# Issuing part of an attention layer's stores and loads from ScalarE's and GpSimd's queues in place of SyncE's

## The chip, the cores and the metric

The kernel runs on one core of one Trainium2 chip. The metric is the device time of one execution in microseconds (us); runs of this kernel took 2020.54 to 2025.85 us, with a median of 2025.57 us. Lower is better. Five engines with an instruction queue each work side by side: PE (TensorE, matrix products), DVE (VectorE), ACT (ScalarE), POOL (GpSimd) and SP (SyncE). An instruction queue is worked through in order: an instruction that waits holds up all that stand behind it on its engine. A transfer between the chip's HBM and the on-chip SBUF (a DMA) is started by an instruction on one of the queues and then runs by itself; whoever needs its data waits for its semaphore.

## What is computed

A stream of 1024 tokens with 1024 channels, float32, goes through two layers: an mLSTM layer (A) and a dilated attention layer (B), each followed by a residual and a layer norm. The change lies in layer B (and in the store of layer A's result that B's end reads). Layer B, from the reference, cut:

```python
def dilated_attention_layer(x, w_in, w_out, kv_blocks, slopes):
    proj = x @ w_in
    q_all = proj[..., :N_GROUPS_B * INNER_B].reshape(bsz, s, N_GROUPS_B, HEADS_B, HEAD_DIM_B)
    z = proj[..., N_GROUPS_B * INNER_B:]
    for g, (window, dilation) in enumerate(GROUPS_B):   # (128, 1), (512, 4), (2048, 16)
        qb = to_residue_blocks(q_all[:, :, g], dilation)
        kb, vb = kv_blocks[g]
        o, lse = dilated_block_attention(qb, kb, vb, dilation, window // dilation, slopes)
        outs.append(from_residue_blocks(o, bsz, s, dilation))
        lses.append(from_residue_blocks(lse, bsz, s, dilation))
    wts = jax.nn.softmax(jnp.stack(lses), axis=0)
    o = jnp.sum(wts[..., None] * jnp.stack(outs), axis=0).reshape(bsz, s, INNER_B)
    y = o.astype(x.dtype) * jax.nn.silu(z)
    return y @ w_out
...
        x = layer_norm(ALPHA * x + y, ln_g[layer], ln_b[layer])
```

There are 8 heads of 128 channels and three groups `g`, each with its own queries, keys and values. The three groups' outputs are merged with weights that come from their softmax denominators.

## The kernel before

Layer A takes the first 850 to 900 us, layer B the rest. Layer B's work is written as loops: `quad` 0 and 1 (heads 0 to 3, and 4 to 7), inside it the group `g` 0 to 2, inside it the head `h`.

Each float32 product is made by three matmuls (L97, L98, L99) on operands that are split into a high and a low part: ACT casts the high part (L92) and DVE subtracts it to get the low part (L93). The projections also go through a Strassen scheme, whose sums are made by DVE (L224, L230, L243, L247, L260, L261) and ACT (L1210 and others). So PE depends at every step on ACT's L92, DVE's L93 and DVE's L230.

The parts that the change touches, each with the tile or the HBM buffer that it moves:

- `layer_a_out` (L1001, L1050): stores layer A's normalized rows into `x1` (buffer `dx` in the order's rows), for layer B's residual.
- `residual(tb)` (L1079 to L1084): loads a block of `x1`, scales it, and stores it back.
- `values` (L1110, L1134): stores the values of a quad to `vn` (`dn`), and loads them back, regrouped, or for quad 1.
- `attend` (L1351): the attention of one head and one group. ACT copies its result out of PSUM into one tile, always the same buffer (L1346 or L1349, two copies), and the tile is stored to `og` (`dg`): 24 stores.
- `factors` (L1360 to L1368) and `merge` (L1383 to L1403): after a head's third group, softmax statistics go to HBM (`ds`), come back as six small loads, are turned into merge factors on DVE and ACT with 8 partitions, and are stored as `f` (`df`, L1403).
- `fetch` (L1405): loads the head's gate `z` (`dz`), the three `og` and the three `f`, each `f` row broadcast to 128 partitions (L1415). `combine` (L1424 to L1428, DVE) multiplies and adds them; `weigh` stores the result to `y2` (`dy`, L1461). For head 3 `by_group` (L1431) does this one group at a time.
- `gates` (L1476): stores the gate halves to `z2` (`dz`).

Weights come through `quarters` (L177) into two raw tiles that are used in turn, so that a weight load waits until DVE's L93 has read its tile for the last time. The output weights come at the end (L1544), with the loads of `y2` (L1546) beside them.

All transfers are issued from SP's queue, 640 in the whole program. The order of each engine's instructions isn't written out by hand: a scheduler lays them out with a simulated timeline when the program is built, within the data dependences and a few `issue_after` hints. So a change of the issuing queue also moves other instructions. SP and ACT share eight completion semaphores for their transfers, which are used in turn; a transfer that gets one again waits for that one's earlier transfer. Transfers of POOL have eight of their own.

Of the kernel before, what the change touches and what calls it, by code (L numbers as in the profile page):

```python
# [18 lines left out]
P = 128  # L19
SEQ = 1024  # L20
# [40 lines left out]
class Kernel:  # L61
# [887 lines left out]
    def layer_a_out(self):  # L949
# [36 lines left out]
        def norm(tbs):  # L986
            n = len(tbs)
            mv, x = self.variances([stats[tb] for tb in tbs])
            rstd = self.rstd(x, n, "ra")
            nb = self.t(self.cp, [P, n], tag="lnb1", bufs=4)  # L990
            V.scalar_tensor_tensor(nb, mv[:, :, 0], -1.0, rstd, op0=ALU.mult, op1=ALU.mult)
            for i, tb in enumerate(tbs):
                r, ri, ni = rows[tb], rstd[:, i:i + 1], nb[:, i:i + 1]
                if i % 2:
                    V.tensor_scalar(r, r, ri, ni, op0=ALU.mult, op1=ALU.add)
                else:
                    A.activation(r, r, AF.Identity, bias=ni, scale=ri)


                if tb >= 4:  # L1000
                    nc.sync.dma_start(self.dram["x1", tb], r)  # L1001

        def transposes(tbs, banks):

# [16 lines left out]
        for half in range(2):  # L1021
# [3 lines left out]
            for c in range(NC_A - tail):  # L1025
                y, w = stream(c, half), weights(c)

                late = c < 3 + half
                for i in range(3 if late else 4):
                    block(ps, i, c, y, w)  # L1030
                if late:
                    first.append((c, y, w))
                if c == 2 + half:
                    if half:
                        transposes((0, 1, 2, 3), Ring(6, 7))
                    else:
                        self.a_tail()
                    ps.append([self.bank(6 + dm) for dm in range(2)])
                    for part in first:
                        block(ps, 3, *part)  # L1040
                    if half:
                        gain, shift = self.ln_params(0, 12, 39)

                if half and c in (5, 6):
                    with self.tc.issue_after(self.last_split.ins):
                        self.x1[("11", "12")[c - 5]]
                if half and 7 <= c < 11:
                    with self.tc.issue_after(self.last_split.ins):
                        self.scale_row(rows[c - 7], gain, shift)
                    nc.sync.dma_start(self.dram["x1", c - 7], rows[c - 7])  # L1050
            if half:

                whs, wls, yhl = Ring(20, 21, 22, 23), Ring(24, 25, 26, 27), Ring(16, 17, 18, 19)
# [15 lines left out]
    def layer_b(self):  # L1069
# [9 lines left out]
        def residual(tb):  # L1079

            r = self.slot(52)
            nc.sync.dma_start(r, self.dram["x1", tb])
            self.scale_row(r, *gain0)
            nc.sync.dma_start(self.dram["x1", tb], r)  # L1084

        jt = self.const("jt", [P, 384], tag="k1")
        jt2 = self.const("jt2", [P, P], tag="k3")
# [9 lines left out]
        def values(g, quad):  # L1097
# [28 lines left out]
            def done(half, i, aps):  # L1126
# [4 lines left out]
                    v[half] = to[half, i]  # L1131
                if i or g:
                    for j, t in enumerate(to[half, i]):
                        nc.sync.dma_start(natural(rows(i, half))[:, 2 * j:2 * j + 2], t)  # L1134
                if g and i == 0:
                    load(half)

# [138 lines left out]
        def attend(h, g, sp, v):  # L1276
# [67 lines left out]
            for bank in range(2):  # L1344
                if g == 0:
                    A.copy(o[:, 512 * bank:512 * bank + 512], po[bank])  # L1346
                else:
                    r = 4 if g == 1 else 8
                    A.copy(o.rearrange("p (i r) -> p r i", r=r)[:, r // 2 * bank:r // 2 * bank + r // 2],  # L1349
                           po[bank].rearrange("p (r i) -> p r i", r=r // 2))  # L1350
            nc.sync.dma_start(self.dram["og", h, g], o)  # L1351

        def factors(h, stat):

# [49 lines left out]

        def fetch(h, accs, os, fbs, z=None):  # L1405

            os_ = [self.slot(accs if g == 0 else os) for g in range(3)]
            fbs_ = [self.slot(fbs) for _ in range(3)]
            if z is None:
                z = self.slot(os)  # L1410
                nc.sync.dma_start(z, self.dram["z2", h])
            for g in range(3):
                nc.sync.dma_start(os_[g], self.dram["og", h, g])
            for g in range(3):
                nc.sync.dma_start(fbs_[g], self.dram["f", h][g:g + 1, :].to_broadcast([P, SEQ]))  # L1415
            return os_, fbs_, z

        def combine(os_, fbs_, z, n=1):
# [12 lines left out]
        def by_group(h, acc, o, fb):  # L1431

            tiles = {}

            def load(g):
                tiles[g] = self.slot(o if g else acc), self.slot(fb)
                nc.sync.dma_start(tiles[g][0], self.dram["og", h, g])
                nc.sync.dma_start(tiles[g][1], self.dram["f", h][g:g + 1, :].to_broadcast([P, SEQ]))

            def step(g):  # L1440
                t, acc = tiles[g][0], tiles[0][0]
# [4 lines left out]
                    load(g + 1)  # L1446
                    return
                z = self.slot(fb)
                nc.sync.dma_start(z, self.dram["z2", h])
# [6 lines left out]
        def weigh(h, fetched):  # L1456

            with self.tc.issue_after(self.last_split.ins):
                acc = combine(*fetched)
            if h < 6:  # L1460
                nc.sync.dma_start(self.dram["y2", h], acc)  # L1461
            return acc

        gain0 = []
# [1 line left out]
        def gates(c2, slots, banks=ones, sz=None):  # L1466
# [4 lines left out]
            def done(half, i, aps):  # L1471
# [220 lines left out]
```

## Time and profile before

| | before |
|---|---|
| runs, us | 2020.54, 2025.57, 2025.85 |
| median, us | 2025.57 |
| profiled execution, us | 2023.8 |
| its span (first to last instruction), us | 2022.0 |
| mean granted TensorE clock | 0.996 of full speed |
| transfers, mean | 145 GB/s |

Busy time is given as a share of the span; PE's, DVE's, ACT's and POOL's shares and the windows of layer B are shown in the prediction. In the rows there, a tile in SBUF is written `s`, one in PSUM `b`, an HBM buffer begins with `d`, an input with `in_`; `x` and a number count instructions. In a row of the timeline the columns are start, duration, engine, line, operation, what it writes and reads, and, in brackets, how long the engine was idle before it and what ended that. `SPq` is SP's queue issuing a transfer. In a row of waits the columns are the total in us, the number of times, and the longest. A row of a window holds its length and then, for PE, PE's weight loads, DVE, ACT and POOL, the busy us and the instructions, then the granted clock, the share of the transfer engines and GB/s.

### The profile page before, as it was taken

How to read it: one execution, taken by the hardware profiler on the slowest of the kernel's cores; microseconds unless marked ns; L12 is line 12 of the kernel's file. 1: busy time of each engine (PE TensorE's matmuls, PEld its weight loads, DVE VectorE, ACT ScalarE, POOL GpSimd, SP SyncE). 2: the span in 40 equal slices, each digit the busy share in tenths (PEclk: the TensorE clock that was granted, in tenths of full speed). 3: DMA queues.
4: the chain of work that ended last, by engine and by line, in shares of the span. 5: the costliest groups of instructions: out<-in, count | busy, mean ns of one | idle time of the engine just before them, and what ended most of it. 6: DMA issues, size and time to landing. Idle time of an engine off the chain costs nothing. (4 is left out here: it accounts for less than half of the span.)

```text
span 2022.0 us, 26727 instructions
## 1 busy us (share of the span) xinstructions
PE 1969.0 (97%) x9576; PEld 1631.2 (81%) x9576; DVE 1451.8 (72%) x2867; ACT 1010.7 (50%) x2008; POOL 154.0 (8%) x127
## 2 busy tenths in 40 slices
PE   8999999999999999999999999999999999999897
PEld 6778888788888888878788888878877888888686
DVE  8778787675577776457867765776679877757878
ACT  5455555535645543343524542565554566765531
POOL 0110000012145343000000000000000000000000
PEclk9999999999999999999999999999999999999999
DMA  4345465456754543516121143224156322123753
GB/s 169 138 162 198 160 221 181 148 166 222 280 203 163 192 163 117 183 62 231 52 73 63 53 146 105 84 84 146 64 210 210 115 94 84 63 84 108 261 199 125
DMA packets 113148, 292.26 MB, mean 145 GB/s; under 512 B 13236, under 2 KB 31092, under 8 KB 113016
## 3 DMA queue, kind: packets, MB, share of 16 engines
q1 hardware_dynamic: 113016, 290.56, 41.1%
q8 instruction: 75, 1.23, 0.3%
q14 instruction: 57, 0.47, 0.1%
HBM read 202.13 MB, written 88.39 MB: 144 GB/s over the span
## 5 line engine op out<-in xcount | busy, mean ns | idle before, releaser
L98 PE MATMUL b<-s,s 128*128 128x512 f32 (+3 forms) x2720 | 1035.5, 382 | 3.0 <-DVE s L93 3.0
L97 PE MATMUL b<-s,s 128*128 128x512 f32 (+2 forms) x2720 | 1010.6, 386 | 28.0 <-ACT s L92 18.6
L99 PE MATMUL b<-s,s 128*128 128x512 f32 (+3 forms) x2720 | 1023.0, 383 | 4.9 <-DVE s L93 4.5
L92 ACT CAST s<-s 128x512 fp32r<-128x512 f32 (+3 forms) x706 | 436.5, 638 | 544.9 <-PE b L99 276.0
L93 DVE TENSOR_TENSOR s<-s,s 128x512 fp32r<-128x512 f32 (+3 forms) x702 | 508.2, 739 | 276.2 <-ACT s L92 272.6
L97 PEld LDWEIGHTS b<-s,s 128*128 128x128 f32 x2720 | 511.9, 188 | 134.6 <-ACT s L92 27.6
L99 PEld LDWEIGHTS b<-s,s 128*128 128x128 f32 x2720 | 511.1, 188 | 105.7 <-DVE s L93 10.2
L98 PEld LDWEIGHTS b<-s,s 128*128 128x128 f32 x2720 | 512.8, 189 | 99.3 <-DVE s L93 5.2
L230 DVE TENSOR_TENSOR s<-s,b 128x512 f32<-128x512 f32 x144 | 98.1, 682 | 37.8 <-PE b L99 35.6
L1273 ACT ACTIVATE s<-s,nmax 128x128 f32<-128x128 f32 (+1 forms) x192 | 84.3, 441 | 27.7 <-DVE nmax L1271 27.5
L224 DVE TENSOR_TENSOR s<-s,b 128x512 f32<-128x512 f32 x96 | 65.1, 680 | 19.9 <-PE b L99 16.4
L93 DVE TENSOR_TENSOR s<-b,s 128x512 fp32r<-128x512 f32 (+1 forms) x96 | 51.7, 553 | 33.9 <-ACT s L92 30.0
L558 DVE SCALAR_TENSOR_TENSOR s<-s,c_convw,s 128x512 f32<-128x512 f32 (+3 forms) x96 | 71.4, 755 | 3.1 <-ACT s L555 2.8
L802 ACT ACTIVATE s<-s,k 128x128 f32<-128x128 f32 x144 | 47.2, 392 | 42.2 <-DVE s L93 18.7
L243 DVE TENSOR_TENSOR s<-s,s 128x512 f32<-128x512 f32 x48 | 33.0, 688 | 42.9 <-DMA s<-in_w_xm 15.1
L1269 DVE CUSTOM_DVE_ANT_0 s<-b,k 128x128 f32<-128x128 f32 (+1 forms) x192 | 57.2, 346 | 3.5 <-PE b L99 3.2
L92 ACT CAST s<-b 128x512 fp32r<-128x512 f32 (+1 forms) x96 | 43.9, 480 | 21.9 <-PE b L99 14.5
L310 DVE TENSOR_TENSOR s<-s,s 128x1024 f32<-128x1024 f32 x32 | 40.1, 1253 | 20.1 <-DMA s<-in_w_o 9.9
L314 DVE TENSOR_TENSOR s<-s,b 128x512 f32<-128x512 f32 x80 | 50.7, 680 | 5.0 <-PE b L99 3.7
L1220 DVE SCALAR_TENSOR_TENSOR s<-s,s 128x512 fp32r<-128x512 f32 x48 | 42.3, 883 | 10.1 <-ACT s L1219 9.6
L761 POOL TENSOR_TENSOR s<-s 128x512 fp32r<-128x512 f32 x32 | 43.4, 1369 | 76.3 <-ACT s L760 68.8
L1287 PE MATMUL b<-c_ident,s 128*128 128x128 f32 x280 | 46.3, 277 | 2.0 <-ACT s L1273 1.9
(185 smaller groups left out, 1527.9 us busy)
## 6 DMA issues: line engine op xcount, KB each, us to landing
s<-in_w_qk SPq DMA_DIRECT2D x48, 512.0 KB
s<-in_w_out SPq DMA_DIRECT2D x40, 512.0 KB
dp<-s SPq DMA_DIRECT2D x32, 512.0 KB
s<-dp SPq DMA_DIRECT2D x32, 512.0 KB
s<-in_w_z SPq DMA_DIRECT2D x24, 512.0 KB
s<-in_w_v SPq DMA_DIRECT2D x24, 512.0 KB
dg<-s SPq DMA_DIRECT2D x24, 512.0 KB
s<-dg SPq DMA_DIRECT2D x24, 512.0 KB
```

The source lines that it names most:

```text
L92: self.nc.scalar.copy(h, src)
L93: self.last_split = (l_eng or self.nc.vector).tensor_tensor(l, src, f(h), op=ALU.subtract)
L97: mm(ps, lh, rh, start=start, stop=False, skip_group_check=skip)
L98: mm(ps, lh, rl, start=False, stop=False, skip_group_check=skip)
L99: mm(ps, ll, rh, start=False, stop=stop, skip_group_check=skip)
L224: V.tensor_tensor(o, p, q, op=add)
L230: V.tensor_tensor(o, p[lane][rows], q[lane][rows], op=add)
L314: V.tensor_tensor(o, p, q, op=add)
L558: V.scalar_tensor_tensor(u[i][:, lo:o + 512], xm[i][:, lo - s:o + 512 - s], convw[:, c, 3 - s:4 - s], u[i][:, lo:o + 512], op0=ALU.mult, o ...
L802: A.activation(E[:, i * P:i * P + P], src[:, i * P:i * P + P], AF.Exp, bias=self.bias[:, hd, ig, j:j + 1])
L1269: V.tensor_tensor_reduce(out=dst, in0=sc, in1=bias, op0=ALU.add, op1=ALU.max, scale=1.0, scalar=-3e38, accum_out=mx[:, b:b + 1])
L1273: self.last_exp = A.activation(res[b][0], res[b][0], AF.Exp, bias=nm[:, b:b + 1], accum_out=stat[:, 1, g, b:b + 1])
```

## The change

Layer B's stores, and the loads that wait for them, leave SP's queue. The `og` stores go to ACT's queue (24 transfers); the `x1`, values, `z2` and `y2` stores, the loads of `x1` in `residual`, of the values, and the fetches of `z`, `og` and `f` go to POOL's (106 transfers). The weights, the small tables of `factors` and `merge`, the fetch for head 7, and all that belongs to the end of the kernel stay on SP. In the new file the lines behind L1406 have a number higher by one. SP has 674 rows before and 544 now, POOL 132 and 238.

```diff
@@ layer_a_out
-                    nc.sync.dma_start(self.dram["x1", tb], r)
+                    nc.gpsimd.dma_start(self.dram["x1", tb], r)
...
-                    nc.sync.dma_start(self.dram["x1", c - 7], rows[c - 7])
+                    nc.gpsimd.dma_start(self.dram["x1", c - 7], rows[c - 7])
@@ layer_b, residual
-            nc.sync.dma_start(r, self.dram["x1", tb])
+            G.dma_start(r, self.dram["x1", tb])
             self.scale_row(r, *gain0)
-            nc.sync.dma_start(self.dram["x1", tb], r)
+            G.dma_start(self.dram["x1", tb], r)
@@ values
-                    nc.sync.dma_start(t, grouped(rows(quad, half))[:, 2 * j:2 * j + 2])
+                    G.dma_start(t, grouped(rows(quad, half))[:, 2 * j:2 * j + 2])
...
-                        nc.sync.dma_start(natural(rows(i, half))[:, 2 * j:2 * j + 2], t)
+                        G.dma_start(natural(rows(i, half))[:, 2 * j:2 * j + 2], t)
@@ attend
-            nc.sync.dma_start(self.dram["og", h, g], o)
+            A.dma_start(self.dram["og", h, g], o)
@@ fetch
+            queue = G if h < 7 else nc.sync
...
-                nc.sync.dma_start(z, self.dram["z2", h])
+                queue.dma_start(z, self.dram["z2", h])
             for g in range(3):
-                nc.sync.dma_start(os_[g], self.dram["og", h, g])
+                queue.dma_start(os_[g], self.dram["og", h, g])
             for g in range(3):
-                nc.sync.dma_start(fbs_[g], self.dram["f", h][g:g + 1, :].to_broadcast([P, SEQ]))
+                queue.dma_start(fbs_[g], self.dram["f", h][g:g + 1, :].to_broadcast([P, SEQ]))
@@ by_group: its four transfers, in the same way
-                nc.sync.dma_start(tiles[g][0], self.dram["og", h, g])
+                G.dma_start(tiles[g][0], self.dram["og", h, g])
...
@@ weigh
-                nc.sync.dma_start(self.dram["y2", h], acc)
+                G.dma_start(self.dram["y2", h], acc)
@@ gates
-                    nc.sync.dma_start(self.dram["z2", 2 * c2 + i][:, 512 * half:512 * half + 512], o)
+                    G.dma_start(self.dram["z2", 2 * c2 + i][:, 512 * half:512 * half + 512], o)
```

The scheduler's order moves with it. Three places follow; a name is a tile (`s`, `b`) or a buffer, with its number in the program.

On DVE, where head 5 is combined while head 6's projection and the last gate's splits run. `s_2665`, `s_2666` and `s_2667` are the three groups' outputs, `s_2668` and `s_2669` broadcast factors; `s_2715` is a Strassen sum that PE's next product reads, `s_2722` and `s_2745` are low parts. Before:

```order
L93 TENSOR_TENSOR s_2722_16445<-s_2710_16336,s_2722_16445 128x512
L1424 TENSOR_TENSOR s_2665_16080<-s_2665_16080,s_2668_16083 128x1024
L1359 COPY s_2694_16258<-b_2693_16256 48x128
L230 TENSOR_TENSOR s_2715_16342<-s_2715_16342,b_2714_16341 128x512
L93 TENSOR_TENSOR s_2745_16567<-s_2738_16558,s_2745_16567 128x512
L1424 TENSOR_TENSOR s_2666_16081<-s_2666_16081,s_2669_16084 128x1024
L1424 TENSOR_TENSOR s_2667_16082<-s_2667_16082,s_2670_16085 128x1024
L230 TENSOR_TENSOR s_2715_16342<-s_2715_16342,b_2713_16340 128x512
```

And now:

```order
L230 TENSOR_TENSOR s_2715_16342<-s_2715_16342,b_2714_16341 128x512
L93 TENSOR_TENSOR s_2722_16445<-s_2710_16336,s_2722_16445 128x512
L1425 TENSOR_TENSOR s_2665_16080<-s_2665_16080,s_2668_16083 128x1024
L93 TENSOR_TENSOR s_2745_16567<-s_2738_16558,s_2745_16567 128x512
L1425 TENSOR_TENSOR s_2666_16081<-s_2666_16081,s_2669_16084 128x1024
L230 TENSOR_TENSOR s_2715_16342<-s_2715_16342,b_2713_16340 128x512
L1425 TENSOR_TENSOR s_2667_16082<-s_2667_16082,s_2670_16085 128x1024
```

The first multiplication with a factor (L1424, now L1425) stood ahead of the first L230 and stands behind it now; the second L230 has two of the three multiplications ahead of it, where it had three.

On SP, where head 2's output is fetched (`s_2147`), head 1's result is stored (`dy_88`), and the next projection's weights are loaded (`s_2211`). Before:

```order
L1411 DMA s_2151_12852<-dz_96_161 128x1024
L1351 DMA dg_99_164<-s_2144_12818 128x1024
L1461 DMA dy_88_153<-s_2109_12606 128x1024
L1413 DMA s_2147_12848<-dg_99_164 128x1024
L177 DMA s_2211_13244<-in_w_qk 128x1024
L1476 DMA dz_110_175<-s_2187_13094 128x512
L1403 DMA df_101_166<-s_2138_12784 8x3x128
```

And now:

```order
L1364 DMA s_2138_12784<-ds_100_165 8x128
L1367 DMA s_2138_12784<-ds_100_165 4x4x32 x2
L177 DMA s_2211_13244<-in_w_qk 128x1024
L177 DMA s_2212_13246<-in_w_qk 128x1024
L1403 DMA df_101_166<-s_2138_12784 8x3x128
```

The store of `dg_99`, the store of `dy_88` and the fetch that waits for the first of them no longer stand ahead of the weights; what is left ahead are the small tables.

On ACT, where the same `dg_99` is stored now:

```order
L237 COPY s_2195_13104<-b_2191_13100 128x512
L92 CAST s_2199_13154<-s_2190_13098 128x512
L1349 COPY s_2144_12818<-b_2140_12796 128x4x128
L1351 DMA dg_99_164<-s_2144_12818 128x1024
L92 CAST s_2200_13175<-s_2189_13096 128x512
L1390 ACTIVATE s_2138_12784<-s_2138_12784 8x384
```

The store follows the second copy directly, and a split (L92) of the gate's weights stands behind it.

At the end of the kernel the load of the second layer norm's gain (L945) now stands ahead of head 6's six small loads, which stood ahead of it before; the first load of output weights (L1544, now L1545) follows behind three of them.

More of the change, by code (lines that the diff above doesn't have):

```diff
@@ L1436, in load @@
                 tiles[g] = self.slot(o if g else acc), self.slot(fb)
-                nc.sync.dma_start(tiles[g][0], self.dram["og", h, g])
-                nc.sync.dma_start(tiles[g][1], self.dram["f", h][g:g + 1, :].to_broadcast([P, SEQ]))
+                G.dma_start(tiles[g][0], self.dram["og", h, g])
+                G.dma_start(tiles[g][1], self.dram["f", h][g:g + 1, :].to_broadcast([P, SEQ]))
             def step(g):
@@ L1448, in step @@
                 z = self.slot(fb)
-                nc.sync.dma_start(z, self.dram["z2", h])
+                G.dma_start(z, self.dram["z2", h])
                 V.tensor_tensor(acc, acc, z, op=ALU.mult)
-                nc.sync.dma_start(self.dram["y2", h], acc)
+                G.dma_start(self.dram["y2", h], acc)
             load(0)
@@ L1460, in weigh @@
             if h < 6:
-                nc.sync.dma_start(self.dram["y2", h], acc)
+                G.dma_start(self.dram["y2", h], acc)
             return acc
```

## The prediction

> **What bounds the kernel now.** I read the page's shares first, then the windows of layer B, then the waits of each engine, and last the timeline around PE's gaps.
>
> ```profile
> PE 1969.0 (97%) x9576; PEld 1631.2 (81%) x9576; DVE 1451.8 (72%) x2867; ACT 1010.7 (50%) x2008; POOL 154.0 (8%) x127
> POOL 0110000012145343000000000000000000000000
> q1 hardware_dynamic: 113016, 290.56, 41.1%
> 1000.00:1200.00 200.00, 199.41 (x997) 168.55 (x998) 140.16 (x282) 92.13 (x208) 0.00 (x0) 1.00 0.21 74
> ...
> sum 1172.00, PE 1137.56 PEld 950.36 DVE 850.43 ACT 579.41 POOL 0.00; mean PE 162.51 PEld 135.77 DVE 121.49 ACT 82.77 POOL 0.00
> ```
>
> PE is busy 97% of the span. The change touches layer B, the stretch from 850 to 2022 us, where PE is busy 1137.56 of 1172.00 us: at most 34.4 us of PE's idle time lie there (a little more where a matmul's modelled end covers a gap), and part of that is the last rows of the kernel, after the last matmul. POOL, which gets most of the moved transfers, does nothing after slice 16, so its queue delays no arithmetic. The transfers use 41.1% of the sixteen DMA engines, so the question isn't bandwidth but when each one is issued. In what PE waits for in layer B, and what the others wait for there, these rows matter:
>
> ```profile
> PE b L97 <- ACT s L92: 7.5, 7, 3.2
> PE b L97 <- DVE s L230: 7.2, 5, 2.6
> DVE s L1424 <- DMA s<-df: 23.2, 6, 5.5
> ACT s L92 <- DMA s<-in_w_out: 28.6, 11, 7.0
> ACT s L92 <- DMA s<-in_w_qk: 8.3, 3, 3.5
> ```
>
> PE's own large waits are twelve, 7.5 + 7.2 = 14.7 us together: that is the prize if every late transfer came in time. SP's queue is full of waits, but most are no loss:
>
> ```profile
> SPq L177 <- DVE s L93: 415.2, 54, 19.4
> SPq L1134 <- DVE s L314: 72.8, 10, 40.5
> SPq L1351 <- ACT s L1349: 56.2, 11, 12.4
> SPq L1413 <- DMA dg<-s: 21.1, 7, 4.6
> SPq L1415 <- DMA df<-s: 9.0, 4, 3.5
> ```
>
> L177 loads the weights' quarters. 54 times it is at the head of the queue waiting for DVE's last read of its own buffer, so nothing ahead of it can have delayed it there. The moved instructions block SP for 72.8 us at L1134 and 56.2 us at L1351. The first lies around the values of groups 0 and 1, where PE is busy 199.41 of 200 us in the window 1000:1200: unblocking SP there can give nothing. So I look at PE's gaps one by one.
>
> **The change part by part.** *Merge factors and PE.* A head's `f` is stored (L1403), loaded back broadcast (L1415, three loads), and used by DVE (L1424). Twice that chain stops PE:
>
> ```profile
> 1505.32 0.29 SPq L1403 DMA_DIRECT2D df<-s  x1
> 1508.88 1.28 SPq L1415 DMA_DIRECT2D s<-df  x3
> 1512.93 1.22 DVE L1424 TENSOR_TENSOR s<-s,s 128x1024 f32<-128x1024 f32 x1 [4.57 <-DMA s<-df]
> 1514.07 0.68 DVE L230 TENSOR_TENSOR s<-s,b 128x512 f32<-128x512 f32 x1
> 1514.81 0.50 PE L97 MATMUL b<-s,s 128*128 128x512 f32 x1 [1.98 <-DVE s L230]
> 1883.15 1.27 SPq L1415 DMA_DIRECT2D s<-df  x3
> 1887.10 1.23 DVE L1424 TENSOR_TENSOR s<-s,s 128x1024 f32<-128x1024 f32 x1 [5.41 <-DMA s<-df]
> 1889.16 0.50 PE L97 MATMUL b<-s,s 128*128 128x512 f32 x1 [2.56 <-DVE s L230]
> ```
>
> DVE takes its work in order; L230, whose result PE needs, stands behind the L1424 that waits for `f`. The gaps are 1.98 and 2.56 us, 4.5 together. In the new order of DVE the first multiplication (now L1425) stands behind that L230 and one more L93, so PE gets its operand at once; but the next L230 is still behind the wait. With the same landing time DVE would be done with L1425 where it is done now, and PE, which has some matmuls in hand after the first L230, loses part of the gap only at the second. I take half: −2.3 us; bounds 0 and −4.5.
>
> *The landing time itself.* The row at 1883.15 shows three loads issued by SP in 1.27 us, 0.42 each; the first is used 4.0 us after its issue (1508.88 to 1512.93). What one transfer costs POOL's queue no row shows, since POOL issues none. From below it is SP's 0.42 us; from above the nearest row of POOL work:
>
> ```profile
> L761 POOL TENSOR_TENSOR s<-s 128x512 fp32r<-128x512 f32 x32 | 43.4, 1369 | 76.3 <-ACT s L760 68.8
> ```
>
> 1.37 us, 0.95 more. The first multiplication needs the first load only, so it is 0 to 0.95 us later in each of six heads (head 3 fetches group by group, head 7's loads stay on SP): 0 to 5.7 us if it all reached PE. I take half a microsecond, as SP's row is the nearer in kind, and cover it by the L230 (0.68 us) that now goes ahead: cost 0. Without that cover it is 6 × 0.5 = 3.0 us. By the Trainium skill ("DMA: Bandwidth & Descriptors", section "Specifications") the first byte comes after about 1 µs on GpSimd's path and about 0.6 µs on the path of SP and ScalarE; by that alone the six heads would be 6 × 0.4 = 2.4 us later, an estimate; no run shows it yet, and the sum doesn't use it.
>
> *SP's head of line.* The place where a moved transfer visibly stands ahead of weights that PE then misses:
>
> ```profile
> 1530.44 0.68 DVE L93 TENSOR_TENSOR s<-s,s 128x512 fp32r<-128x512 f32 x1
> 1531.19 0.32 SPq L1413 DMA_DIRECT2D s<-dg  x1
> 1531.60 0.38 SPq L177 DMA_DIRECT2D s<-in_w_qk  x1
> 1537.97 0.62 ACT L92 CAST s<-s 128x512 fp32r<-128x512 f32 x1 [2.47 <-DMA s<-in_w_qk]
> 1538.64 0.50 PE L97 MATMUL b<-s,s 128*128 128x512 f32 x1 [1.54 <-ACT s L92]
> ```
>
> L1413 waits there for a store, and L177 behind it goes at 1531.60. But L177's buffer is last read by the L93 that ends at 1530.44 + 0.68 = 1531.12. Freed of L1413 it goes 0.5 us earlier, not more: −0.5 of the gap's 1.54. The largest gap of all is like it:
>
> ```profile
> 1894.36 0.36 SPq L1413 DMA_DIRECT2D s<-dg  x1
> 1899.09 0.33 SPq L945 DMA_DIRECT2D s<-in_ln_g  x1
> 1899.85 0.32 SPq L1461 DMA_DIRECT2D dy<-s  x1
> 1900.27 1.94 SPq L1544 DMA_DIRECT2D s<-in_w_out  x1
> 1908.67 2.09 ACT L92 CAST s<-s 128x1024 fp32r<-128x1024 f32 x3 [7.02 <-DMA s<-in_w_out]
> 1910.29 0.50 PE L97 MATMUL b<-s,s 128*128 128x512 f32 x1 [3.23 <-ACT s L92]
> ```
>
> Here L1461 goes to POOL, and the output weights could be issued 1900.27 − 1899.85 = 0.4 us earlier. But L945, which stays on SP and waits for ACT until 1899.09, is still ahead of them, and in the new order three small loads of merge factors stand between the two (they were issued before L945). So I put this gap at 0, bounds −3.2 and +2. What is late after this change is thus still L945 and the broadcast `f`.
>
> *Stores on ScalarE.* 24 stores of the attention's output (L1351) go into ACT's order, each right behind the copy that fills the tile.
>
> ```profile
> 1524.77 1.14 ACT L1349 COPY s<-b 128x512 f32<-128x512 f32 x1
> 1525.94 0.32 SPq L1351 DMA_DIRECT2D dg<-s  x1
> 1526.98 0.52 ACT L1390 ACTIVATE s<-s 8x384 f32<-8x384 f32 x1 [1.07 <-DVE s L1389]
> ```
>
> On SP the store takes 0.32 us and starts 0.03 us after the copy's end. On ACT it also holds up the next instruction, which otherwise would follow at once: 0.35 us each, 24 × 0.35 = 8.4 us of ACT. ACT is busy 579.41 of 1172 us there, about half; so half, 4.2 us, falls where ACT would be idle anyway, as in the 1.07 us above. Of the other 4.2 us, what delays a split (L92) that PE waits for counts: PE waits for ACT as often as for DVE, so I take half again, +2.1 us. Bounds: 0, and 8.4 if every one reaches PE.
>
> *The rest.* The x1 stores and residuals, the values' stores and loads, z2 and y2 (L1001, L1050, L1082/1084, L1110, L1134, L1476, L1461) have no reader soon and leave SP, whose weights wait for their own buffers: 0, covered by PE's 199.41 of 200 us above. Their loads on POOL are in one order with the `f` loads, so a store that waits for DVE there can hold a fetch back, as it does on SP now: no change.
>
> **The sum.** −2.3 − 0.5 + 0 + 2.1 = −0.7 us. The profiled execution took 2023.8 us (1.8 around the span of 2022.0), the median of the runs is 2025.57, the lowest 2020.54. Forecast: 2023.8 − 0.7, about 2023 us. About 0.3%, 6 us, can be told from no change: faster means below 2019.5, slower above 2031.6.
>
> **The rivals.** *(A) The late transfers all go.* PE's two chains of gaps close, at 1514 and 1889 (4.5 us), at 1538 (1.5) and at 1910 (3.2), as SP is never blocked and DVE no longer stands before PE: −9.2 us, and −12 with the shorter gaps behind the same rows; 2012 to 2015 us. For it: each of these gaps names a transfer on SP. Against: L945 stays, and L177's buffer. *(B) Slower: `f` lands later than DVE's new order covers.* Place: the first L1425 of each of six heads, with the next L230 behind it. If a load costs POOL 1.37 us, the second of three, whose multiplication also stands ahead of an L230, is issued 2 × 0.95 = 1.9 us later than now. It decides from the point where the landing is more than 1.3 us later, the L230 and L93 (0.68 us each) that now go first. Price: at six heads 6 × 1.9 = 11.4 us, less where PE has work in hand (four of the six now), and ACT's stores on PE's path 2 to 8; 2030 to 2040 us. For it: the six waits for `f` are already 23.2 us long. Against: only two of the six reach PE. *(C) SP's issue time was never the bound, and the new queues give nothing:* 2023.8 to 2025.6 us, which stands within the forecast's range. The Trainium skill says the same ("DMA: Bandwidth & Descriptors", section "Issuing engines are not separate DMA queues"): whichever engine issues them, DMAs share the same sixteen engines, and other issuers only save the sequencer's time. The 54 waits of L177 agree with it. Apart from the named places, every engine's order in layer B is arranged anew by the scheduler, and this can move the time by some microseconds either way; it widens each case.
>
> **How the numbers follow.** Forecast with (C), 2019 to 2028 us: 0.44. (A), 2009 to 2019: 0.25. (B), 2028 to 2041: 0.31. Of the forecast's case 0.05 lies below 2019.5; of (A) 0.01 above it; of (B) 0.02 below 2031.6. Faster 0.29, same 0.42, slower 0.29. The likeliest case alone is 2019 to 2028. The range needs most of both rivals: 2010 to 2038 leaves out about 0.05 below and 0.1 above.
>
> **What would show it.** In the changed kernel: DVE's waits of L1425 for `f` (now 23.2 us, six; shorter speaks for A, above 32 for B); PE's waits for L230 (7.2) and for ACT's L92 (7.5: growing to 10 shows the price of the stores); the gap before the output weights (3.2, unchanged by my forecast); the length of a POOL issue against 0.42 us. I am wrong if PE gets new gaps at places not named here, from the new order alone, or if transfers on POOL land several microseconds later.

## The result, and the profile after

Runs of the changed kernel took 2036.80, 2040.38, 2041.03 and 2041.33 us, median 2040.7. With those of the kernel before (2016.81 to 2025.85, median 2023.05) the ratio is 1.0085 (95%: 1.0068 to 1.0101): slower by about 17 us. That is above the predicted range. The profiled execution took 2036.8 us, with a span of 2034.4 and a mean granted clock of 0.993. From the page of after, engines, POOL's slices, and the transfer queues:

```profile
PE 1971.4 (97%) x9576; PEld 1636.6 (80%) x9576; DVE 1451.3 (71%) x2867; ACT 1012.2 (50%) x2008; POOL 214.1 (11%) x233
POOL 0110000012145442000000001000011000000000
q1 hardware_dynamic: 92248, 225.54, 31.9%
q0 software_dynamic: 14496, 52.44, 7.4%
q10 hardware_dynamic: 3456, 12.58, 1.5%
```

The transfers now stand in three queues: q0 for POOL's, q10 for ACT's, q1 for SP's. In the traces SP issued 696 transfers before (not 640, as the part on the kernel before has it) and issues 566 now. PE idles 2034.4 − 1971.4 = 63.0 us, where it idled 2022.0 − 1969.0 = 53.0. Of the span's 12.4 us more, 10.0 are idle time of PE and 2.4 matmuls that took longer (the clock 0.993 after 0.996). Three windows of after, then of before (length, PE, PE's weight loads, DVE, ACT, POOL, clock, transfers):

```profile
1400.00:1600.00 200.00, 190.86 (x948) 158.12 (x947) 153.76 (x340) 105.24 (x216) 19.57 (x35) 0.99 0.42 141
1840.00:1960.00 120.00, 105.12 (x506) 86.92 (x505) 93.79 (x203) 63.15 (x120) 9.55 (x18) 0.94 0.63 223
1960.00:2034.00 74.00, 63.54 (x281) 52.26 (x279) 57.13 (x151) 8.37 (x8) 0.00 (x0) 0.96 0.26 96
```

```profile
1400.00:1600.00 200.00, 194.18 (x959) 161.41 (x958) 154.41 (x342) 104.98 (x215) 0.00 (x0) 0.99 0.41 141
1840.00:1960.00 120.00, 112.50 (x546) 92.29 (x546) 97.40 (x206) 60.25 (x116) 0.00 (x0) 0.99 0.64 230
1960.00:2022.00 62.00, 51.18 (x225) 41.72 (x223) 50.51 (x140) 8.31 (x8) 0.00 (x0) 0.94 0.28 102
```

From 1400 to 1600 us PE idles 9.14 us after 5.82, and from 1840 to the end 25.34 after 18.32: together 10.3 us more, so PE's added idle time lies in the two stretches where heads are merged. In the waits from 850 us on (total, times, longest):

```profile
PE b L97 <- ACT s L92: 14.7, 5, 6.9
PE b L97 <- DVE s L230: 2.1, 4, 0.8
DVE s L1425 <- DMA s<-df: 21.0, 6, 5.8
ACT s L92 <- DMA s<-in_w_out: 35.3, 15, 5.4
POOL s L1416 <- DMA df<-s: 28.7, 4, 14.8
SPq L177 <- DVE s L93: 703.2, 62, 42.2
```

PE's waits for L230 fell from 7.2 to 2.1 us, as the order on DVE promised. Its waits for ACT's L92 doubled from 7.5 to 14.7, most of it in two new gaps, at 1559 and 1956 us:

```profile
1555.70 0.62 ACT L92 CAST s<-s 128x512 fp32r<-128x512 f32 x1 [8.92 <-DVE s L260]
1559.39 0.51 PE L97 MATMUL b<-s,s 128*128 128x512 f32 x1 [4.31 <-ACT s L92]
1931.84 0.26 SPq L1403 DMA_DIRECT2D df<-s  x1
1932.89 0.84 SPq L1545 DMA_DIRECT2D s<-in_w_out  x2
1933.86 1.66 POOL L1416 DMA_DIRECT2D s<-df  x3 [14.81 <-DMA df<-s]
1943.37 1.23 DVE L1425 TENSOR_TENSOR s<-s,s 128x1024 f32<-128x1024 f32 x1 [5.84 <-DMA s<-df]
1954.46 1.99 ACT L92 CAST s<-s 128x1024 fp32r<-128x1024 f32 x2 [5.33 <-DVE s L1425]
1956.50 0.79 PE L97 MATMUL b<-s,s 128*128 128x512 f32 x1 [6.88 <-ACT s L92]
```

Read the last six rows as a chain: head 6's `f` is stored (L1403), SP issues two quarters of the output weights, POOL issues the three loads of `f`, and DVE can use the first 9.51 us after its issue (1933.86 to 1943.37; in the kernel before 6.27, with no wait). Two more multiplications, then ACT casts and PE waits 6.88 us. But the late transfer isn't the whole of it. Head 6's `f` is itself stored 12.5 us later than in the kernel before (1931.84 after 1919.35), and the run p2 below, which has the new order with every transfer on SP, has gaps of 4.34 and 5.53 us at the same two places. SP itself is freer than before: L177 waits 703.2 us for its own buffers, after 415.2.

In the changed kernel, operations that issue a transfer on POOL and on ACT, and the time from issue to landing of L1416 (`f`):

```profile
L1416 POOL DMA_DIRECT2D s<-df x18: 528/528/539, 1477.8 to 1935.0; - x18
DMA to landing us min/median/max: 4.0/7.3/13.4
L1351 ACTq DMA_DIRECT2D dg<-s x24: 326/326/352, 1109.2 to 1935.0; - x24
```

An issue takes POOL 0.53 us and ACT 0.33; the landing takes up to 13.4 us, in which the head's other `f` loads in the same queue have a part.

### The profile page after: what moved, and what is told of

Its sections match the earlier page's. It is cut to its first block, busy times and chain, and to the rows that moved or that the text cites. A ratio compares the mean times of both kernels' runs of the same rounds, so it can differ in the third digit from the quotient of the medians.

```text
span 2034.4 us, 26767 instructions
## 1 busy us (share of the span) xinstructions
PE 1971.4 (97%) x9576; PEld 1636.6 (80%) x9576; DVE 1451.3 (71%) x2867; ACT 1012.2 (50%) x2008; POOL 214.1 (11%) x233
## 3 DMA queue, kind: packets, MB, share of 16 engines
q1 hardware_dynamic: 92248, 225.54, 31.9%
## 5 line engine op out<-in xcount | busy, mean ns | idle before, releaser
L92 ACT CAST s<-s 128x512 fp32r<-128x512 f32 (+3 forms) x706 | 436.9, 637 | 536.7 <-PE b L99 285.2
L230 DVE TENSOR_TENSOR s<-s,b 128x512 f32<-128x512 f32 x144 | 98.1, 682 | 49.1 <-PE b L99 46.3
L1273 ACT ACTIVATE s<-s,nmax 128x128 f32<-128x128 f32 (+1 forms) x192 | 84.4, 441 | 33.9 <-DVE nmax L1271 33.3
L243 DVE TENSOR_TENSOR s<-s,s 128x512 f32<-128x512 f32 x48 | 33.1, 690 | 43.6 <-DMA s<-in_w_qk 14.7
L92 ACT CAST s<-b 128x512 fp32r<-128x512 f32 (+1 forms) x96 | 44.0, 480 | 20.6 <-PE b L99 14.2
L872 POOL TENSOR_TENSOR s<-s,s 128x512 f32<-128x512 f32 x32 | 42.7, 1351 | 64.0 <-DVE s L871 48.8
```

The lines of the kernel that those rows point to most:

```text
L92: self.nc.scalar.copy(h, src)
L230: V.tensor_tensor(o, p[lane][rows], q[lane][rows], op=add)
L1273: self.last_exp = A.activation(res[b][0], res[b][0], AF.Exp, bias=nm[:, b:b + 1], accum_out=stat[:, 1, g, b:b + 1])
```

## The experiments

The change does two things at once: it moves transfers to other queues, and the scheduler, seeing other queues, lays out every engine anew. To hold one still, a kernel was **pinned** to another's order: a table of instruction numbers per engine, and for each two neighbours a dependence that orders the issue and adds no wait.

```python
for a, b in zip(names, names[1:]):
    tc.add_manual_dep(at[b], a, kind, reason="in_order")   # kind: NoSync
```

On each queue the transfers then stand in the order in which they stood in the other kernel; between two queues nothing is fixed. Ratios are to the kernel before, on the same chip; they come from several runs, and the spans of single profiles scatter by some us around them. Rows, waits and landing times come from one profiled execution of each kernel.

### The queues, or the new order

All of the change, in the order of before (p1: the changed kernel, pinned), and no change of queues, in the order of the changed kernel (p2: the kernel before, pinned). The edit is the same for both, with different tables:

```diff
         Kernel(tc, aps, out).build()
+        in_order(tc)
```

> All moved transfers on their new queues, but every other instruction of PE, DVE, ACT and POOL, and the transfers within each queue, held in the order of the kernel before. Theory 'queues' (a transfer from POOL lands later, a store on ACT holds ACT up): the loss is still there, ratio to before 1.006 to 1.010. Theory 'order' (the scheduler's new order, above all head 6's statistics copied behind head 5's combination, so that head 6's factors come 12 us later): the loss is gone, ratio 0.997 to 1.002. Both: in between.

> All transfers on SP as before, but PE, DVE, ACT and SP held in the order of the changed kernel. Theory 'queues': ratio to before 0.997 to 1.002. Theory 'order': ratio 1.005 to 1.010.

p1: 1.0096 (1.0075 to 1.0117). p2: 1.0053 (1.0035 to 1.0070). So the new queues cost about 20 us by themselves. The new order, on the old queue, costs 11 us too, mostly in gaps like those at 1559 and 1956 above, which p2 has at 1565.73 and 1955.60:

```profile
1562.04 0.62 ACT L92 CAST s<-s 128x512 fp32r<-128x512 f32 x1 [10.59 <-DVE s L260]
1565.73 0.80 PE L97 MATMUL b<-s,s 128*128 128x512 f32 x1 [4.34 <-ACT s L92]
1955.60 0.79 PE L97 MATMUL b<-s,s 128*128 128x512 f32 x1 [5.53 <-ACT s L92]
```

So either part alone loses, but the two don't add: on the new queues the new order (1.0085) is no worse than the old (1.0096). And PE's waits for L92 are 14.3 us in p2, with every transfer on SP: a sum like the changed kernel's 14.7 comes from the order alone.

### Which of the moved transfers

Each in the order of before: only the `og` stores on ACT (p3), only POOL's transfers (p4), only the `f` loads on POOL (p5), POOL's transfers without the `f` loads (p6). And, with the scheduler free, the whole change but for the `f` loads (e3).

```diff
  # p3
-            nc.sync.dma_start(self.dram["og", h, g], o)
+            A.dma_start(self.dram["og", h, g], o)
  # p4: the changed kernel, with
-            A.dma_start(self.dram["og", h, g], o)
+            nc.sync.dma_start(self.dram["og", h, g], o)
  # p5: the kernel before, with
-                nc.sync.dma_start(fbs_[g], self.dram["f", h][g:g + 1, :].to_broadcast([P, SEQ]))
+                (G if h < 7 else nc.sync).dma_start(fbs_[g], self.dram["f", h][g:g + 1, :].to_broadcast([P, SEQ]))
  # p6: p4, and e3: the changed kernel, each with
-                queue.dma_start(fbs_[g], self.dram["f", h][g:g + 1, :].to_broadcast([P, SEQ]))
+                nc.sync.dma_start(fbs_[g], self.dram["f", h][g:g + 1, :].to_broadcast([P, SEQ]))
```

(`by_group`'s `f` loads, for head 3, go with the others.)

> The order of the kernel before, only the 24 og stores moved to ACT. My prediction's term: +2.1 us, ratio 1.001; if every store reaches PE, +8.4 us, ratio 1.004. Theory 'order': no more than 1.001.

> The order of the kernel before, the 106 transfers moved to POOL, the og stores left on SP. Theory 'queues' by way of POOL: ratio 1.004 to 1.010, with the first multiplication of each head (L1425) waiting longer for f than the 23.2 us of before, above 32 us. Theory 'order': 0.997 to 1.002.

> The order of the kernel before; only the broadcast loads of f (21 of the 24, all but head 7's) go from SP to POOL. Theory 'f' (POOL's f loads land later, DVE waits in front of what PE needs): most of the 1.1% that all POOL moves cost, ratio 1.006 to 1.011, DVE's waits for f above 32 us. Rival 'the other moves' (the loads of z, og and values, or the stores, are late or crowd the weights): ratio 0.999 to 1.003.

> The order of the kernel before; the moves to POOL without the f loads (85 transfers). Theory 'f': ratio 0.999 to 1.003. Rival 'the other moves': 1.006 to 1.011.

> The changed kernel, f loads back on SP, the scheduler free to order it. It puts head 6's statistics ahead of the small norm load again, as before. Theory 'f' (with the order a consequence of it): ratio 0.998 to 1.002. Rival: it stays above 1.005.

| kernel | ratio | 95% |
|---|---|---|
| p3, og stores on ACT | 1.0003 | 0.9989 to 1.0017 |
| p4, all of POOL's | 1.0110 | 1.0084 to 1.0136 |
| p5, only f on POOL | 1.0053 | 1.0036 to 1.0071 |
| p6, POOL's without f | 1.0015 | 0.9996 to 1.0035 |
| e3, all but f | 1.0011 | 0.9998 to 1.0024 |

The stores on ACT cost nothing that can be told. The `f` loads, 18 transfers and three for head 3 of the 130 moved, cost 11 us alone; without them the kernel is 0.15% (p6) or 0.11% (e3) above the one before, at most 0.35% by the intervals. In e3 only the queue of `f` differs from the changed kernel, and with it the scheduler's order: head 6's `f` is stored at 1914.49 there, and no gaps of 4 us or more stand at the two places. So the changed kernel has its new order as a consequence of where `f` is issued. p5 (+0.53%) and p6 (+0.15%) don't add up to p4 (+1.10%): together they cost about 8 us more than apart (1 to 16 with the three intervals taken as independent). One cause of that is visible, in p4 at head 0:

```profile
1476.61 0.27 SPq L1403 DMA_DIRECT2D df<-s  x1
1481.77 0.56 POOL L1414 DMA_DIRECT2D s<-dg  x1 [5.78 <-ACT s L1273]
1482.37 1.68 POOL L1416 DMA_DIRECT2D s<-df  x3
```

The last `og` load stands ahead of `f` in POOL's queue and still waits, probably for the store that it reads (issued at 1476.08; the row names ACT's L1273 and doesn't tell). So `f` goes 5.76 us after its own store; in the kernel before it was 3.63 (1472.29 to 1475.92). Head 4 is the same (5.32 after 3.73).

In p5 nothing stands ahead of `f` on POOL. The waits of its profile:

```profile
DVE s L1424 <- DMA s<-df: 36.7, 10, 6.6
PE b L97 <- ACT s L92: 10.5, 5, 5.2
PE b L97 <- DVE s L230: 9.7, 4, 4.1
```

The loads are issued, but land later. Head 1 in p5, and then the one row of the kernel before that the prediction doesn't show:

```profile
1507.93 0.29 SPq L1403 DMA_DIRECT2D df<-s  x1
1511.01 0.33 SPq L177 DMA_DIRECT2D s<-in_w_z  x1
1511.98 1.57 POOL L1415 DMA_DIRECT2D s<-df  x3 [33.27 <-DMA df<-s]
1517.59 1.23 DVE L1424 TENSOR_TENSOR s<-s,s 128x1024 f32<-128x1024 f32 x1 [6.61 <-DMA s<-df]
1519.47 0.69 PE L97 MATMUL b<-s,s 128*128 128x512 f32 x1 [4.13 <-DVE s L230]
```

```profile
1510.20 0.43 SPq L177 DMA_DIRECT2D s<-in_w_z  x1
```

Before, a weight quarter (L177) was issued at 1510.20, right behind the three `f` loads at 1508.88: one queue, and `f` stood first. In p5 nothing holds that quarter on SP, and it goes at 1511.01, 0.97 us ahead of the first `f` load. `f` is used 5.61 us after its issue, where it was 4.05, and PE's gap there is 4.13 after 1.98. So a new theory: it is not POOL that is slow; `f` has **lost its place ahead of the weights**, with which it shares the transfer engines. The rival: POOL's path itself is slower.

### Lost place, or slow path

The weight quarter moved ahead of `f` on SP, at heads 1, 2 and 5, with nothing on POOL (p11); `f` on POOL as in p5, with the quarter behind it made to wait until the last `f` load has landed (p12 at six heads, p14 at the five but head 6, whose `f` stays on SP); `f` on ACT's queue in place of POOL's (p13; head 3's `f` stays on SP there). All in the order of before.

```diff
  # p11, SP's order at head 1
+L177 DMA s_2190_13098<-in_w_z 128x1024
 L1415 DMA s_2112_12609<-df_94_159 128x1024
 L1415 DMA s_2113_12610<-df_94_159 128x1024
 L1415 DMA s_2114_12611<-df_94_159 128x1024
-L177 DMA s_2190_13098<-in_w_z 128x1024
  # p12, p14: behind in_order
+    for load, factor in BEHIND:
+        tc.add_manual_dep(at[f"I-{load}"], f"I-{factor}", wait, reason="behind_f")
  # p13
-                nc.sync.dma_start(fbs_[g], self.dram["f", h][g:g + 1, :].to_broadcast([P, SEQ]))
+                (A if h < 7 else nc.sync).dma_start(fbs_[g], self.dram["f", h][g:g + 1, :].to_broadcast([P, SEQ]))
```

> The kernel before, all on SP, its own order, but at heads 1, 2 and 5 the weight load that stands behind the three f loads in SP's queue stands ahead of them. Theory 'overtaking' (f is late on POOL because the weights no longer queue behind it): f is used 1 to 2 us later at these heads though POOL has no part in it, ratio 1.001 to 1.004. Theory 'path' (POOL's own transfers are slower): f not later by more than 0.5 us, ratio 0.999 to 1.001.

> Only the f loads on POOL in the old order, and the next weight load of SP at heads 0, 1, 2, 4, 5 and 6 waits until the last f load has landed, so no weights stand beside them. Theory 'overtaking': first use of f 4.0 to 4.5 us after its issue, most of the 0.53% comes back, ratio 1.000 to 1.003 (less if the weights are then late themselves). Theory 'path': first use stays above 5 us after the issue, ratio 1.004 to 1.007.

> The order of the kernel before, the f loads (but head 7's) issued by ACT. To read landing times: another queue beside SP's, but issued as SP's are. Theory 'path': first use about 4.0 us after the issue at heads 1 and 5, as on SP. Theory 'overtaking': 5 to 6 us, as on POOL. The time itself rises, since ACT waits for f's store ahead of its own work: ratio 1.003 to 1.012.

> As the run with f on POOL and SP's next weight load waiting for it (1.0064), but head 6's f stays on SP and nothing waits there, since in that run the wait I added held head 7's small loads and an output weight in SP's queue for 10 us. Theory 'overtaking': f on POOL by itself is then nearly free, ratio 1.000 to 1.003, no gap of 5 us before the last products of head 7's part. If the path by itself cost the time: 1.004 to 1.007.

From the rows of each timeline, the time from the issue of the first `f` load to DVE's first use of it, in us; at these heads DVE waits for it, so that it is the landing, except at head 2 of after, where DVE came later and 5.90 is only an upper bound:

| head | before | after | p5 (POOL) | p11 (SP, weights first) | p12 (POOL, weights wait) | p13 (ACT) |
|---|---|---|---|---|---|---|
| 1 | 4.05 | 4.85 | 5.61 | 5.99 | 4.31 | 5.45 |
| 2 | 3.86 | 5.90 | 6.49 | 5.11 | 4.14 | 6.04 |
| 5 | 3.95 | 5.30 | 5.15 | 6.01 | 4.40 | 4.26 |
| ratio | 1 | 1.0085 | 1.0053 | 1.0029 | 1.0064 | 1.0019 |

Head 1 in p11, then in p12:

```profile
1510.01 0.33 SPq L177 DMA_DIRECT2D s<-in_w_z  x1
1510.70 1.27 SPq L1415 DMA_DIRECT2D s<-df  x3
1516.69 1.23 DVE L1424 TENSOR_TENSOR s<-s,s 128x1024 f32<-128x1024 f32 x1 [6.71 <-DMA s<-df]
1518.57 0.79 PE L97 MATMUL b<-s,s 128*128 128x512 f32 x1 [4.34 <-DVE s L230]
```

```profile
1506.97 1.56 POOL L1415 DMA_DIRECT2D s<-df  x3 [30.95 <-DMA df<-s]
1511.28 1.23 DVE L1424 TENSOR_TENSOR s<-s,s 128x1024 f32<-128x1024 f32 x1 [5.28 <-DMA s<-df]
1513.16 0.50 PE L97 MATMUL b<-s,s 128*128 128x512 f32 x1 [1.87 <-DVE s L230]
1513.80 0.33 SPq L177 DMA_DIRECT2D s<-in_w_z  x1
```

p11 makes the lateness of p5 with all of it on SP: 5.99 us and a gap of 4.34, by one swap. p12 takes it away with `f` on POOL: 4.31 us and a gap of 1.87. For the landing at these heads both are measured: place in the queue, 1.3 to 2.1 us (p11 less before); POOL's path, 0.26 to 0.45 us (p12 less before; there nothing of SP's follows `f` at once, so the path may cost a little more). One quarter is 512 KB, 1.5 us at the 345 GB/s that after reached from 1934 to 1943.3 us, so the swap costs about one quarter's transfer, an estimate.

For the time it is settled in part. p11 is 1.0029 (1.0016 to 1.0043): three swaps alone make about 6 (3 to 9) of the 11 us of p5. But p12, where `f` lands in time, is 1.0064 (1.0046 to 1.0082), and p14 1.0041 (1.0027 to 1.0055): by what was expected of them, these times speak for the slow path, though the landing times speak against it. In both the added wait holds SP itself: in p12 at head 6 the output weights come late, and ACT's L92 waits 10.71 us for them at 1938.96; in p14 the quarter at head 1 goes at 1516.74 (before: 1510.20), and PE's waits for L92 are 12.2 us (before: 7.5). In these two runs a wait in another queue was no substitute for a place in the same one. What remains of p5 beside the three swaps can't be split further from these runs; one visible part is its head 6, whose loads share the transfer engines with the output weights (DMA share 1.03 from 1937 to 1943 us) and are used 5.7, 9.1 and 12.3 us after the first issue.

p13 is 1.0019 (1.0007 to 1.0032), below the 1.003 that was expected at least. Issued by ACT on a third queue, `f` is late at heads 1 and 2, where SP issues a quarter 0.39 and 0.19 us ahead of it, and on time at head 5 (4.26), where the quarter goes 2.23 us behind it. In that trace's packet records the first packet of `f` starts 1.93 and 2.72 us after its issue at heads 1 and 2, and 0.98 at head 5; in the kernel before it was 0.95 to 1.08. So what delays the landing is the weights nearby, with POOL or without it.

In the changed kernel `f` is late at head 5 though its first load is issued 0.44 us ahead of the quarter. The rows, and then each queue's packets, MB and share of the transfer engines, from 1890.5 to 1892.5 us (POOL's queue alone) and from 1892.5 to 1894:

```profile
1889.26 1.60 POOL L1416 DMA_DIRECT2D s<-df  x3 [5.18 <-DMA df<-s]
1889.70 0.36 SPq L177 DMA_DIRECT2D s<-in_w_z  x1
1894.56 1.22 DVE L1425 TENSOR_TENSOR s<-s,s 128x1024 f32<-128x1024 f32 x1 [4.89 <-DMA s<-df]
```

```profile
q0 software_dynamic: 103, 0.42, 100.8%
```

```profile
q1 hardware_dynamic: 75, 0.31, 53.8%
q0 software_dynamic: 40, 0.10, 35.5%
```

POOL's queue had moved 0.42 MB, less than its first load (0.52), when the weights came in with 0.31 MB to its 0.10. Being issued first did not protect `f` here, on a queue of its own.

### Can an order cover it?

The L230 that PE needs put ahead of the waiting L1424 at heads 1 and 5, queues as before (p7, the prediction's first term by itself); needed work put first at heads 0, 1, 2, 4 and 5 (p8); p8's order with `f` on POOL (p10); p4 with `f` ahead of the `og` load in POOL's queue (p9).

```diff
  # p7, DVE's order of before at head 1, and the same at head 5
+L230 TENSOR_TENSOR s_2160_12870<-s_2160_12870,b_2159_12869 128x512
 L1424 TENSOR_TENSOR s_2109_12606<-s_2109_12606,s_2112_12609 128x1024
-L230 TENSOR_TENSOR s_2160_12870<-s_2160_12870,b_2159_12869 128x512
  # p8 and p10, the same place
-L1424 TENSOR_TENSOR s_2109_12606<-s_2109_12606,s_2112_12609 128x1024
 L230 TENSOR_TENSOR s_2160_12870<-s_2160_12870,b_2159_12869 128x512
 L1359 COPY s_2138_12784<-b_2137_12782 48x128
 L93 TENSOR_TENSOR s_2196_13105<-s_2189_13096,s_2196_13105 128x512
+L1424 TENSOR_TENSOR s_2109_12606<-s_2109_12606,s_2112_12609 128x1024
...
  # p9, POOL's order at head 0
-L1414 DMA s_2075_12368<-dg_85_150 128x1024
 L1416 DMA s_2076_12369<-df_87_152 128x1024
 L1416 DMA s_2077_12370<-df_87_152 128x1024
 L1416 DMA s_2078_12371<-df_87_152 128x1024
+L1414 DMA s_2075_12368<-dg_85_150 128x1024
```

> The kernel before, all on SP, in its own order, but with the L230 that PE waits for put ahead of the first multiplication with f at heads 1 and 5. My prediction's term: 2.3 us less, bounds 0 and 4.5; ratio 0.9978 to 1.0. If the gap only moves to the next L230: 1.000.

> The kernel before, all on SP, its own order, but on DVE at heads 0, 1, 2, 4 and 5 the sums, low parts and the next head's statistics that PE's products wait for are put ahead of the multiplications that wait for f, and the third multiplication behind the second L230. If waiting DVE is what passes the late f on to PE: ratio 0.994 to 0.998, more than the two swaps (0.9978). Rival, the gap only moves to the next product: 0.998 to 1.001.

> As the run with all moves to POOL in the old order (1.011), but in POOL's queue the three f loads stand ahead of the last og load at heads 0, 1, 4, 5 and 6. Theory 'queue head' (part of the lateness is that og load, which waits for its own store, in front of f): ratio 1.005 to 1.008, the time from f's store to its loads back under 4 us. Rival (the path itself): 1.010 to 1.012.

> Only the f loads on POOL, with DVE's order of the run that puts needed work first. My prediction held that 0.5 us of later landing is covered by such an order: then it costs nothing against that run (difference of ratios below 0.0015). If f comes 2 us later per head than DVE's order can cover, the difference stays at 0.003 to 0.005.

| kernel | ratio | 95% |
|---|---|---|
| p7, L230 first at two heads | 0.9978 | 0.9964 to 0.9992 |
| p8, needed work first at five | 0.9986 | 0.9974 to 0.9998 |
| p10, p8 with f on POOL | 1.0054 | 1.0033 to 1.0074 |
| p9, p4 with f ahead of og | 1.0093 | 1.0076 to 1.0111 |

p7 gains about 4.4 us (1.6 to 7.3). It has the lowest ratio of all, some 1% below the changed kernel (0.9978 beside 1.0085). PE's waits for L230 are down from 7.2, and the gaps of 1.98 and 2.56 us at heads 1 and 5 are gone (the profiled execution, 2026.31 us, was the slowest of ten, so the row shows the place and not the gain):

```profile
PE b L97 <- DVE s L230: 3.8, 3, 2.9
```

p8's longer list gains no more than p7. p10 answers the question: even with the needed work ahead of every wait, `f` on POOL costs 1.0054 − 0.9986, about 14 us (9 to 19, with the intervals taken as independent). This order didn't hide the lateness. p9 overlaps p4 and settles nothing: `f` was issued sooner at head 0 (4.91 us after its store in place of 5.76), but an L177 still went ahead of it.

### The output weights

The prediction left 3.2 us at the gap before the output weights, since L945 stays ahead of them on SP. p7, with L945 and L946 of layer B on POOL (p15):

```diff
-        self.nc.sync.dma_start(g, self.a["ln_g"][layer:layer + 1, :].to_broadcast([P, D]))
-        self.nc.sync.dma_start(b, self.a["ln_b"][layer:layer + 1, :].to_broadcast([P, D]))
+        q = self.nc.gpsimd if layer else self.nc.sync
+        q.dma_start(g, self.a["ln_g"][layer:layer + 1, :].to_broadcast([P, D]))
+        q.dma_start(b, self.a["ln_b"][layer:layer + 1, :].to_broadcast([P, D]))
```

> The kernel before with the two swaps of L230 (0.9978), and the two loads of the last norm's gain and shift on POOL, so that the wait of L945 for ACT no longer stands ahead of the output weights on SP. My prediction held this gap to be L945's doing: if so, 3.2 us less, ratio 0.994 to 0.9975. If the weights are late for another reason: 0.9975 to 0.999.

0.9988 (0.9975 to 1.0002): no gain over p7. The output weights were issued at 1899.40 us, hardly sooner than before (1900.27): SP's store of `y2` (L1461 in the kernel before) stood at 1898.65. In this kernel a gap of 2.95 us appeared at 1959.63. But the gap before the output weights is missing from p7's profile already, so p15 had nothing to gain there, and whether L945 made it stays open.

## Why the prediction was wrong

- **The forecast** was no change, 2023, and the rival on the other side (B) held 0.31. The direction and the place of B came true: `f` lands later, at the merges of the heads. That its price, 2030 to 2040, came near the 2040.7 was luck: it rested on an issue of 1.37 us, and an issue on POOL took 0.53.
- **The step that failed** is "*The landing time itself*": "I take half a microsecond, … and cover it by the L230 … that now goes ahead: cost 0". Both halves fell. The size came from what an issue costs the queue (0 to 0.95 us); an issue on POOL is 0.53 us, only 0.1 above SP's 0.42, but the landing became 0.8 us later at head 1 and 1.35 at head 5 of the changed kernel (1.2 to 2.6 at heads 1, 2 and 5 of p5), and at head 6 the first use came 9.51 us after the issue. And the cover didn't hold: with the needed work first, p10 lost about 14 us against p8. The term of 0 measured 11 us with `f` alone (p5). What the runs showed in place of an issue's length is the neighbourhood of a weight load: 1.3 to 2.1 us of landing at three heads (p11). How all of p5's 11 us come of that stays open, as p12 and p14 gave no time back.
- **Why it was missed.** The prediction asked what a transfer costs the queue that it goes to, and what it frees on the queue that it leaves. It didn't ask what it had been ahead of there. The row `1508.88 … L1415` was among its rows on the merge factors, and the weights that stood right behind it were not. B's threshold (a landing 1.3 us later) was just met at head 5 (1.35), perhaps at head 2 (at most 2.0), and not at head 1 (0.8).
- **The new order** stood in the prediction as "some microseconds either way" and had no term in the sum. On the old queues it costs 11 us by itself (p2). The sign "new gaps at places not named here, from the new order alone" came true there, at 1565.73 and 1955.60 us.
- "**a store that waits for DVE there can hold a fetch back, as it does on SP now: no change**" failed too. On POOL, behind the `og` load, `f` went about 2 us later after its store at heads 0 and 4 of p4, and in the changed kernel 5.98 and 5.77 us passed there from store to load, after 3.63 and 3.73. What this costs by itself p9 didn't settle.
- **Merge factors and PE**, −2.3 with bounds 0 and −4.5: right in kind. p7 gained 4.4 us (1.6 to 7.3), which agrees with the −2.3 and with the bound of −4.5.
- **Stores on ScalarE**, +2.1 us: p3 gave +0.03% (−0.11 to +0.17%, which is −2.2 to +3.4 us), so neither the term nor a cost of nothing is excluded. The growth of PE's waits for L92 to 14.7 us, named as the sign of that price, is no such sign: p2 has 14.3 with every transfer on SP.
- **SP's head of line and the output weights**, −0.5 and 0: e3, with all the moved transfers but `f` off SP, gained nothing (1.0011). The gap at 1910 us did close in the changed kernel, and a larger one came at 1956.50; but it is missing from the profile of p7 too, with every transfer on SP, so its closing says nothing of the queues.
- **The signs**: L1425's waits for `f` were 21.0 us, below 32, and thus pointed away from B while `f` landed later. The sum was a poor sign. Of the 23.2 us before, 5.5 were head 7's, whose loads stay on SP and which has no such wait now, so that the other heads went from 17.7 to 21.0; and the scheduler had put other work ahead of the waiting instruction. In the pinned p4 and p5, in the old order, the same waits are 38.6 and 36.7.
- **The Trainium skill.** The estimate from "DMA: Bandwidth & Descriptors", section "Specifications" (0.4 us more to the first byte on GpSimd's path) agrees with p12's 0.26 to 0.45 us. The rule that other issuers only save the sequencer's time (same page, "Issuing engines are not separate DMA queues") agrees with e3, p6 and p3, which gained nothing. What bears on the loss stands in "Queues, rings and completion order" of that page: within one ring descriptors start in order, and each transfer engine takes turns between the queues that have work. p11 agrees with the first half: a place in one queue was worth 1.3 to 2.1 us. Head 5 of the changed kernel agrees with the second: 0.31 MB of weights, issued later on another queue, moved while `f` moved 0.10.

## What to carry to other kernels

In these runs the order of transfers in one queue was a priority (1.3 to 2.1 us of landing, p11), so before moving a transfer to another queue, look at which large loads stood behind it there: an urgent small one that others wait for should stay ahead of them in the same queue. One sum of waits didn't show the loss (21.0 us after 23.2), since the scheduler had moved other work; pin the order to tell queues from order. And an instruction that waits for a transfer should have what the bounding engine needs ahead of it, which was the one gain found here (p7).

## What the runs showed that was not expected

- An execution order that suits one set of queues is bad for another: the new order cost 0.53% on the old queue and nothing that can be told on the new ones (p2; and 1.0085 for the changed kernel beside p1's 1.0096).
- Making a weight load wait for another queue's transfer cost about what the lateness had cost that it removed: p12 1.0064 and p14 1.0041 beside p5's 1.0053, with overlapping intervals.
- A broadcast load of 512 KB took from 4.0 to 13.4 us to land within one kernel, at a mean use of the transfer engines of 31.9 + 7.4 + 1.5 = 40.8%: the mean says nothing of the stretch in which it is issued.
